# Attention with filler matmuls: when the fillers' inputs are loaded and split, where the softmax sums are gathered and exchanged, and when sums are evicted

## The chip, the cores and the metric

The kernel runs on one core of a Trainium2 chip. The metric is device time in microseconds (us) of one execution; the time before is the median of three runs. Five engines work side by side, each through its own instructions in order: PE (TensorE, matmuls), DVE (VectorE), ACT (ScalarE), POOL (GpSimd) and SP, which here only issues DMAs. They wait for one another by semaphores.

## The reference

One decoder layer of width 1024 over 2048 tokens, in float32:

```python
h = rms_norm(x, g_norm) * (1 + scale) + shift
x_rnn, z_rnn, q, k, v, z_attn, g_r, g_a = split(h @ w_in)
hr = rg_lru(causal_depthwise_conv(x_rnn), ...)              # linear recurrence over tokens
y_rnn = (hr * silu(z_rnn)) @ w_out_rnn
o = dilated_attention_mixture(rope(q), rope(k), v)          # 8 heads of 128
y_attn = (o * silu(z_attn)) @ w_out_attn
merged = sigmoid(g_r + b_r) * y_rnn + sigmoid(g_a + b_a) * y_attn
out = rms_norm(x + gate * (merged @ w_o), g_final)
```

Three causal attentions with (window, dilation) of (128, 1), (512, 4) and (2048, 16) are evaluated per head and added with the weights of their softmax sums: the result is one softmax over the three key sets together.

## The kernel before, in words

Float32 products are made of fast matmuls on split numbers: an operand is split into a rounded high part and the low part that is left, and `mm3` (L151) issues three matmuls (high by high, high by low, low by high). The high part is made by ACT (`hi_act`, L157) or DVE (`hi_dve`, L160), the low part by POOL (`lo_pool`, L163) or DVE (`lo_dve`, L166). A split so costs one instruction on each of two engines.

The first 1400 us or so compute the projections, the recurrence and the queries, keys and values. Then comes the attention stage, the place of the change, whose instruction order is written by hand (`tc.manual_schedule()`); behind it the last products follow, in an order that a scheduler sets.

**Units and slots.** The sequence is taken in two halves, f = 0 and f = 1, with 8 heads each: 16 heads in all. A head has six units (`ORDER`, L1392): four `c` units for the two wide windows, two `w` units for the narrow one. The loop runs over slots; slot s computes on PE the scores of unit s (tile `sc`, PSUM, two buffers), the transposes of unit s - 7 (`pT`, PSUM, two buffers), and the sums over values of unit s - 8 (`o`). In between:

- DVE adds the mask and takes the row minimum of the negated scores (L1470), ACT takes exponentials and sums them (L1471); minima and sums go into the small tile `st`.
- When a head's six units are scored, the two layouts of rows (g = 0 for `c`, g = 1 for `w`) must see each other's sums. `gather` (L1619) spreads `st` into `sm` on DVE, `exchange` is one small matmul `sc<-sm,msk` on PE into an `sc` buffer, `maxima`, `exponentials` and `weights` make the weights `M` on DVE and ACT. `scale` (L1535) then multiplies a unit's probabilities by `M` on ACT, in the slot before its transposes.
- The transposed probabilities are split into `pth` and `ptl` (L157 or L160, and L166). The sums in `o` are multiplied by the gate `zt` on their way out of PSUM by DVE (`evict`, L1594 for `c`, L1614 for `w`).

Within a slot the pieces are issued in this order: HEAD, scores and softmax steps, SOFTMAX, fillers, EXCHANGE, fillers, WEIGHTS, transposes, fillers, sums, TAIL. `at(slot, place, fn)` puts a function into one of the named places.

**Fillers.** Two output projections are cut into jobs of 64 steps (`steps`, L1707): jobs 0 to 3 are the recurrence's four column blocks, 4 to 7 the attention's. A step is one `mm3` with 512 columns into `pj`; eight steps (k = 0 to 7) make one tile, eight tiles (m = 0 to 7) a job. Each slot is owed 3.6 steps in the first half and 3.1 in the second, and `spend` issues whole steps until less than the allowance `left` + 1 is owed. A job needs eight inputs `y` of 128x512. `load_y` brings one from DRAM into a ring of four raw buffers (`R0` to `R3`), `split_y` makes `yh` and `yl` (nine buffers each). Loads of inputs 0 to 3 of the next job are issued at steps 44 to 50 of a job, those of 4 to 7 at steps 56 to 59, each for a buffer that the split of the input four before it frees; all eight splits are issued at steps 55 to 62. Weights come in halves of 512 KB (`S<-wD`).

Of the kernel before, what the change touches and what calls it, by code (L numbers as in the profile page):

```python
# [10 lines left out]
F32 = mybir.dt.float32  # L11
F32R = mybir.dt.float32r
# [77 lines left out]
def decoder_block(ctx, tc, x, c, positions, g_norm, w_mod, b_mod, w_in, b_gate, conv_w, conv_b,  # L90
# [4 lines left out]
    def T(pool, shape, dt, tag, **kw):  # L95
        cnt[0] += 1
        return pool.tile(shape, dt, tag=tag, name=f"{tag}_{cnt[0]}", **kw)
# [58 lines left out]
    def hi_act(o, i):  # L156
        nc.scalar.activation(o, i, AF.Copy)  # L157
# [182 lines left out]
    def load_yd(ys, n, k):  # L340
        x = n_y[0]
        n_y[0] += 1
        t = T(pR, [P, CH], F32, f"R{x % 4}")
        nc.sync.dma_start(t[:], ys[k * P : (k + 1) * P, n * CH : (n + 1) * CH])
        Y0[ys is yaT, n, k] = t
# [1054 lines left out]
    def at(slot, place, fn, *args):  # L1400
        plan.setdefault((slot, place), []).append((fn, args))
# [5 lines left out]
    class Head:  # L1407
# [208 lines left out]
            return evict  # L1616


        def gather(self):  # L1619

            self.sm = T(ap_, [P, 2, 4, 2, 8], F32, "sm")
            for g in range(2):
                nc.vector.tensor_tensor(
                    self.sm[:, g], self.st[:, :, g].rearrange("p t b n -> p t (b n)").unsqueeze(1).broadcast_to([P, 4, 2, 8]),
                    qm.unsqueeze(2).unsqueeze(3).broadcast_to([P, 4, 2, 8]), ALU.mult)

        def exchange(self):
            self.px = T(sc, [P, 2, 4, 2, 4, 2], F32, "sc")
# [52 lines left out]
        def enlist(self, B):  # L1681
            for c, (ld, s, place) in enumerate(((5, 2, HEAD), (5, 2, SOFTMAX), (4, 1, HEAD), (3, 0, HEAD))):
                at(B - ld, TAIL, self.load_kq, c)
                at(B - s, place, self.split_kq, c)
            for i, s in enumerate((B, B + 2)):
                at(s, HEAD, self.window_queries, i)
            e = B + NU
            at(e, HEAD, self.gather)
            at(e, EXCHANGE, self.exchange)
            at(e, EXCHANGE, self.maxima)  # L1690
            at(e, EXCHANGE, self.exponentials)
            at(e, WEIGHTS, self.weights)
            for u, (kind, x) in enumerate(ORDER):
                s = B + u + LAG
                at(s - 1, TAIL, self.scale, kind, x)
                at(s - 1, TAIL, self.split_v if kind == "c" else self.split_v1, x)
                at(s - 3, TAIL, self.load_v if kind == "c" else self.load_v1, x)
            e = B + NU + LAG
            at(B + LAG - 1, TAIL, self.load_gate)
            at(e, TAIL, self.merge, 1)  # L1700
            at(e + 1, TAIL, self.merge, 3)
            at(e + 2, TAIL, self.store)
# [4 lines left out]
    def steps(jobs):  # L1707

        tiles = [(j, m) for j in range(len(jobs)) for m in range(KT)]
        Y, G = {}, {}  # L1710

        def load_w(x):

            if x < 2 * len(tiles):
                assert x == n_w[0]
                j, m = tiles[x // 2]
                if not whole:
                    load_wd(jobs[j][0], m, x % 2)
                    return

                n_w[0] += 1
                W[x] = T(pS, [P, 2, KH, P], F32R, f"S{x % 4}")
                t = T(whole[0], [P, KH, P], F32, "wr", bufs=3)
                rows = slice(x % 2 * KH * P, (x % 2 + 1) * KH * P)
                nc.sync.dma_start(t[:], (w_out_rnn, w_out_attn)[jobs[j][0]][0, rows, m * P : (m + 1) * P]
                                  .rearrange("(k p) m -> p k m", p=P))
                hi_act(W[x][:, 0], t[:])
                (lo_dve if x % 2 else lo_pool)(W[x][:, 1], t[:], W[x][:, 0])

        def load_y(j, k):  # L1730
            if j < len(jobs):
                w, ys, n = jobs[j]
                if ys is oT and (n, k) == (2, KT - 1):

                    Y0[False, n, k] = last_head[0].zt[:, 0].rearrange("p r j -> p (r j)")
                    return
                assert ys is yaT or (n // 2, k, n % 2) in stored
                load_yd(ys, n, k)

        def split_y(j, k):  # L1740
            if j < len(jobs):
                Y[j, k] = yh, yl = [T(fl, [P, CH], F32R, tag, bufs=NY) for tag in ("yh", "yl")]
                w, ys, n = jobs[j]
                t = Y0.pop((ys is yaT, n, k))
                hi_act(yh[:], t[:])
                (lo_dve if k % 2 else lo_pool)(yl[:], t[:], yh[:])

        def load_g(t):
            j, m = tiles[t]
            w, ys, n = jobs[j]  # L1750
            at_ = slice(m * P, (m + 1) * P), slice(n * CH, (n + 1) * CH)
            G[t] = []
            for src in (grT,) if ys is yaT else (gaT, mrT):
                g = T(fl, [P, CH], F32, "fg", bufs=4)
                nc.sync.dma_start(g[:], src[at_])
                G[t].append(g)

        def evict(t, ps):
            g = G[t]
            nc.vector.tensor_tensor(g[0][:], ps[:], g[0][:], ALU.mult)  # L1760
            if len(g) > 1:
                nc.vector.tensor_tensor(g[0][:], g[0][:], g[1][:], ALU.add)  # L1762

        def store(t):
            j, m = tiles[t]
            w, ys, n = jobs[j]
            nc.sync.dma_start((mrT if ys is yaT else meT)[m * P : (m + 1) * P, n * CH : (n + 1) * CH], G.pop(t)[0][:])

        for k in range(KT):
            split_y(0, k)  # L1770
        yield
        last = None
        for t, (j, m) in enumerate(tiles):
            ps = T(pj, [P, CH], F32, "pj")
            for k in range(KT):
                if k % KH == 1:

                    load_w(2 * t + k // KH + 3)
                if k == 1 and t:
                    evict(t - 1, last)  # L1780
                if k == 3:
                    load_g(t)
                if k == 7 and t:
                    store(t - 1)
                wt = W[2 * t + k // KH]
                yh, yl = Y[j, k]
                mm3(ps[:], wt[:, 0, k % KH, :], wt[:, 1, k % KH, :], yh[:], yl[:], first=k == 0, last=k == KT - 1)
                if k % KH == KH - 1:
                    W.pop(2 * t + k // KH)

                step = m * KT + k
                if step in range(KT * KT - 20, KT * KT - 12, 2):
                    load_y(j + 1, (step - KT * KT + 20) // 2)
                if step == KT * KT - KT - 1:
                    split_y(j + 1, 0)
                if step >= KT * KT - KT and k + 1 < KT:
                    if k + 4 < KT:
                        load_y(j + 1, k + 4)
                    split_y(j + 1, k + 1)
                yield  # L1800
            last = ps
        evict(len(tiles) - 1, last)
        store(len(tiles) - 1)
# [13 lines left out]
    with tc.manual_schedule():  # L1817
        units = []
        for g in range(2 * H):
            hd = Head(g // H, g % H)  # L1820
            hd.enlist(NU * g)
            units += [(hd, u) for u in ORDER]
        last_head = [hd]
        owed = 0.0
        first = min(s for s, _ in plan)
        end = max(s for s, _ in plan) + 1
        for s in range(first, max(end, len(units) + LAG + 1)):
            rate = FILL[0] if s < NU * H + LAG else FILL[1]
            owed += rate + (MORE if 0 <= s <= NU else 0.0)

            run(s, HEAD)
            softmax = None
            if 0 <= s < len(units):
                hd, u = units[s]
                softmax = hd.scores(*u)
            if softmax:
                softmax()
            run(s, SOFTMAX)
            owed = spend(fill, owed, rate * 2 / 3)
            run(s, EXCHANGE)  # L1840
            owed = spend(fill, owed, rate / 3)
            run(s, WEIGHTS)
            if 0 <= s - LAG < len(units):
                hd, u = units[s - LAG]
                hd.transposes(*u)
            owed = spend(fill, owed, 0.0)
            if 0 <= s - LAG - 1 < len(units):
                hd, u = units[s - LAG - 1]
                evict = hd.sums(*u)
                if evict:  # L1850
                    at(s + 1, HEAD, evict)
            run(s, TAIL)
        owed = spend(fill, (NB + 2) * KT * KT - n_steps[0], 0)
    pools.close("ap", "sc", "pT", "po")
# [84 lines left out]
```

## Time and profile before

| | before |
|---|---|
| median of three runs (range) | 2293.89 us (2292.89 to 2299.7) |
| profiled execution, its own time | 2291.72 us |
| its span, first to last instruction | 2289.9 us |
| PE busy, share of the span | 2223.0 us, 97% |
| DVE | 1388.3 us, 61% |
| ACT | 1232.7 us, 54% |
| POOL | 993.6 us, 43% |
| granted PE clock, mean | 0.991 |

The profile is of one execution. A row of the timeline reads: start, duration, engine, line, operation, out<-in tiles, shapes, number of instructions merged; in brackets the engine's idle time before it and what ended it. PE overlaps matmuls, so the distance between two starts says what a matmul costs, not its duration. An engine that waits inside a merged row, or that is held up in the middle of an instruction, counts as busy.

### The profile page before, as it was taken

What the parts mean: (1) busy time and instruction counts of PE and PEld (TensorE: products, weight loads), DVE (VectorE), ACT (ScalarE), POOL (GpSimd) and SP (SyncE); (2) the same over time, 40 slices, a digit from 0 to 9 for tenths busy, and PEclk for the clock granted to TensorE, in tenths of its full rate; (3) what the DMA queues carried; (4) which work ended last, traced back from release to release, by engine and by line L of the source; (5) the groups of instructions that cost most, each with busy time, mean ns of one, the idle gap of its engine ahead of it and who ended that gap; (6) DMA issues with size and microseconds to landing.
All of it is one profiled execution on the core that took longest, in us unless ns stands there. A gap on an engine that the chain in (4) does not pass through costs nothing.

```text
span 2289.9 us, 34038 instructions
## 1 busy us (share of the span) xinstructions
PE 2223.0 (97%) x11455; PEld 1863.0 (81%) x11455; DVE 1388.3 (61%) x2380; ACT 1232.7 (54%) x2397; POOL 993.6 (43%) x742
## 2 busy tenths in 40 slices
PE   9999999999999999999999999999999998989998
PEld 5997788888777988888888877788888897868887
DVE  5668888768457555545445253567667777667443
ACT  3647768668433436557546312567677777533211
POOL 2367676767556432222222022446556556332100
PEclk9999999999999999999999999999999999999999
DMA  8367887887998458887888999889888888898542
GB/s 279 92 201 254 273 295 265 288 282 257 309 274 265 141 188 270 269 283 252 276 271 265 319 330 316 263 263 273 266 247 251 241 255 233 241 308 278 165 129 92
DMA packets 429011, 573.40 MB, mean 250 GB/s; under 512 B 72134, under 2 KB 293026, under 8 KB 427812
## 3 DMA queue, kind: packets, MB, share of 16 engines
q1 hardware_dynamic: 390996, 451.47, 64.4%
q10 hardware_dynamic: 37648, 119.70, 13.5%
q8 instruction: 91, 1.49, 0.3%
q14 instruction: 84, 0.69, 0.1%
q0 software_dynamic: 192, 0.05, 0.0%
HBM read 357.18 MB, written 213.91 MB: 249 GB/s over the span
## 4 chain that ended last, share of the span: by engine, by line
PE 56%; DMA 8%; DVE 3%; SPq 2%; ACT 2%; issue 1%; POOL 1%; ACTq 0%; POOLq 0%; DVEq 0%
PE pj L149 12%; PE X L149 8%; PE pq L149 8%; PE V L149 7%; PE o L149 4%; PE Z L149 4%; PE sc L149 4%; PE W L149 4%; PE Y L149 3%; DMA R<-in_w_in_dram 2%; DMA S<-sD 1%; PE pT L1555 1%; PE pg L149 1%; PE pT L1568 1%; DMA meT<-fg 1%
## 5 line engine op out<-in xcount | busy, mean ns | idle before, releaser
L149 PE MATMUL pj<-yh,S 128*128 128x512 f32 x1024 | 369.6, 405 | 6.6 <-DMA S<-wD 4.6
L149 PE MATMUL V<-T,S 128*128 128x512 f32 x1344 | 332.3, 396 | 6.4 <-DVE t L449 3.8
L149 PE MATMUL X<-T,S 128*128 128x512 f32 x1344 | 332.0, 396 | 3.8 <-ACT u L382 2.1
L163 POOL TENSOR_TENSOR S<-R,S 128x512 fp32r<-128x512 f32 x168 | 253.3, 1515 | 164.5 <-ACT S L157 145.2
L149 PEld LDWEIGHTS V<-T,S 128*128 128x128 f32 x1344 | 253.7, 189 | 67.1 <-issue 3.7
L149 PEld LDWEIGHTS X<-T,S 128*128 128x128 f32 x1344 | 253.4, 189 | 64.7 <-ACT u L382 2.8
L149 PEld LDWEIGHTS pj<-yh,S 128*128 128x128 f32 x1024 | 194.2, 190 | 44.3 <-DVE fg L1762 4.3
L149 PE MATMUL pj<-yl,S 128*128 128x512 f32 x512 | 202.5, 395 | 1.4 <-POOL yl L163 0.9
L1471 ACT ACTIVATE pp<-pp,st 128x256 f32<-128x256 f32 (+3 forms) x256 | 133.9, 524 | 107.4 <-DVE st L1470 106.7
L163 POOL TENSOR_TENSOR S<-s,S 128x512 fp32r<-128x512 f32 x84 | 131.9, 1571 | 127.4 <-ACT S L157 89.6
L149 PE MATMUL W<-T,S 128*128 128x512 f32 x672 | 165.8, 395 | 0.0
L149 PE MATMUL Z<-T,S 128*128 128x512 f32 x672 | 165.7, 395 | 0.0
L149 PE MATMUL Y<-T,S 128*128 128x512 f32 x672 | 165.5, 395 | 0.0
L163 POOL TENSOR_TENSOR s<-R,s 128x512 fp32r<-128x512 f32 x32 | 44.0, 1377 | 252.2 <-ACT s L157 193.9
L149 PEld LDWEIGHTS Y<-T,S 128*128 128x128 f32 x672 | 126.5, 188 | 29.4
L149 PEld LDWEIGHTS W<-T,S 128*128 128x128 f32 x672 | 126.1, 188 | 29.8 <-issue 0.9
L149 PEld LDWEIGHTS Z<-T,S 128*128 128x128 f32 x672 | 126.3, 188 | 29.3
L166 DVE TENSOR_TENSOR ptl<-pT,pth 128x384 fp32r<-128x384 f32 (+1 forms) x160 | 97.8, 628 | 65.7 <-ACT pth L157 63.5
L944 DVE SCALAR_TENSOR_TENSOR xc<-xr,par,xc 128x512 f32<-128x512 f32 x96 | 97.7, 1018 | 50.8 <-ACT xc L938 48.5
L1535 ACT ACTIVATE pp<-pp,M 128x256 f32<-128x256 f32 (+3 forms) x256 | 118.0, 523 | 9.0 <-DVE M L1659 9.0
L1470 DVE CUSTOM_DVE_ANT_0 pp<-sc,msk 128x256 f32<-128x256 f32 (+3 forms) x256 | 104.9, 449 | 25.6 <-PE sc L149 23.1
L157 ACT ACTIVATE S<-R 128x512 fp32r<-128x512 f32 x168 | 102.2, 621 | 21.8 <-DMA R<-in_w_in_dram 13.7
(331 smaller groups left out, 4763.4 us busy)
## 6 DMA issues: line engine op xcount, KB each, us to landing
sD<-S ACTq DMA_DIRECT2D x196, 512.0 KB, 4.0
S<-sD SPq DMA_DIRECT2D x196, 512.0 KB, 5.2
S<-wD SPq DMA_DIRECT2D x99, 512.0 KB, 5.7
R<-in_w_in_dram SPq DMA_DIRECT2D x136, 256.0 KB, 4.1
wD<-s ACTq DMA_DIRECT2D x64, 256.0 KB, 5.1
T<-in_w_mod_dram SPq DMA_DIRECT2D x8, 1024.0 KB, 11.4
vN<-ev SPq DMA_DIRECT2D x64, 128.0 KB, 1.9
zaT<-ev SPq DMA_DIRECT2D x32, 256.0 KB, 4.9
```

The costliest lines, as they stand in the source:

```text
L149: nc.tensor.matmul(o, lhsT=l, rhs=r, start=st, stop=sp, **kw)
L157: nc.scalar.activation(o, i, AF.Copy)
L163: nc.gpsimd.tensor_tensor(o, i, h.bitcast(F32), ALU.subtract)
L166: nc.vector.tensor_tensor(o, i, h.bitcast(F32), ALU.subtract)
L944: nc.vector.scalar_tensor_tensor(xc, xr[:, i : i + CH], cw(i), xc, ALU.mult, ALU.add)
L1470: nc.vector.tensor_tensor_reduce(pdst, s_ps, mask, 1.0, 3e38, ALU.add, ALU.min, m_)
L1471: nc.scalar.activation(pdst, pdst, AF.Exp, bias=m_, scale=-1.0, accum_out=l_)
L1535: nc.scalar.activation(pp, pp, AF.Copy, scale=w)
L1555: nc.tensor.transpose(pt[:, c0 + j * P : c0 + (j + 1) * P], pp[i][:, k * P : (k + 1) * P], ident)
L1568: nc.tensor.transpose(pt[:, c * P : (c + 1) * P], pp[:, half * P : (half + 1) * P], ident)
```

## The change

1. Inputs 0, 5, 6 and 7 of each job but the first are loaded straight into the buffer of their low part (`yl`); ACT reads it and writes `yh`, and the low part is made in place. Inputs 1 to 4 still go through `R`, so each raw buffer is used once in a job.
2. Loads of inputs 0 to 4 are issued at steps 40 to 48 of the job before, those of 5, 6, 7 in its last tile, behind k = 4, 5, 6. Splits 0 to 4 stay where they were; splits 5, 6, 7 move into the first tile of their own job, behind k = 0, 2, 3.
3. The eight low parts of job 0 are all made by DVE (four were POOL's).
4. `gather` takes one layout at a time: `w` behind the softmax steps of the head's last slot, `c` at the start of the next slot, where both were.
5. The evictions of `o` move from HEAD of the next slot to behind its softmax steps.
6. Three quarters of a slot's fillers come ahead of the exchange and the rest behind it; none are left between transposes and sums. Before, it was a third at each of the three places.

```diff
-            at(e, HEAD, self.gather)
+            at(e - 1, SOFTMAX, self.gather, 1)
+            at(e, HEAD, self.gather, 0)
...
+        def new_y(j, k):
+            Y[j, k] = [T(fl, [P, CH], F32R, tag, bufs=NY) for tag in ("yh", "yl")]
+            return Y[j, k]
...
-                load_yd(ys, n, k)
+                if k in (1, 2, 3, 4):
+                    load_yd(ys, n, k)
+                else:
+                    yh, yl = new_y(j, k)
+                    nc.sync.dma_start(yl[:].bitcast(F32), ys[k * P : (k + 1) * P, n * CH : (n + 1) * CH])
...
-                t = Y0.pop((ys is yaT, n, k))
-                hi_act(yh[:], t[:])
-                (lo_dve if k % 2 else lo_pool)(yl[:], t[:], yh[:])
+                t = Y0.pop((ys is yaT, n, k), None)
+                yh, yl = Y.get((j, k)) or new_y(j, k)
+                t = yl[:].bitcast(F32) if t is None else t[:]
+                hi_act(yh[:], t)
+                (lo_dve if k % 2 or not j else lo_pool)(yl[:], t, yh[:])
...
-                if step in range(KT * KT - 20, KT * KT - 12, 2):
-                    load_y(j + 1, (step - KT * KT + 20) // 2)
+                if step in range(KT * KT - 24, KT * KT - 14, 2):
+                    load_y(j + 1, (step - KT * KT + 24) // 2)
                 if step == KT * KT - KT - 1:
                     split_y(j + 1, 0)
-                if step >= KT * KT - KT and k + 1 < KT:
-                    if k + 4 < KT:
-                        load_y(j + 1, k + 4)
-                    split_y(j + 1, k + 1)
+                if m == KT - 1:
+                    if k < 4:
+                        split_y(j + 1, k + 1)
+                    elif k < KT - 1:
+                        load_y(j + 1, k + 1)
+                if j and m == 0 and k in (0, 2, 3):
+                    split_y(j, 5 + (k + 1) // 2)
...
             run(s, SOFTMAX)
-            owed = spend(fill, owed, rate * 2 / 3)
+            owed = spend(fill, owed, rate / 4)
             run(s, EXCHANGE)
-            owed = spend(fill, owed, rate / 3)
+            owed = spend(fill, owed, 0.0)
...
-                    at(s + 1, HEAD, evict)
+                    at(s + 1, SOFTMAX, evict)
```

How the instructions move is shown at three places, as the two kernels issue them.

ACT at the change from job 0 to job 1 (`yh` are the splits, `pp<-pp,M` the scaling that the next transposes wait for, `pp,st` the exponentials, `vh` and `kq` splits of values and keys). Before:

```order
L157 ACTIVATE yh_13356<-R_2301_13271 128x512
L157 ACTIVATE yh_13363<-R_2305_13283 128x512
L157 ACTIVATE yh_13372<-R_2311_13300 128x512
L157 ACTIVATE yh_13397<-R_2322_13354 128x512
L1535 ACTIVATE pp_12971<-pp_12971,M_13075 128x128
L1535 ACTIVATE pp_12971<-pp_12971,M_13075 128x256
L157 ACTIVATE vh_13409<-vraw_13239 128x256
```

And in the changed kernel:

```order
L157 ACTIVATE yh_13349<-R_2273_13137 128x512
L1535 ACTIVATE pp_12971<-pp_12971,M_13085 128x128
L1535 ACTIVATE pp_12971<-pp_12971,M_13085 128x256
L157 ACTIVATE vh_13399<-vraw_13240 128x256
L157 ACTIVATE kq_12675<-kraw_13242 128x512
L1471 ACTIVATE pp_13413,st_13050<-pp_13413,st_13050 128x128
L1471 ACTIVATE pp_13413,st_13050<-pp_13413,st_13050 128x256
L157 ACTIVATE yh_13356<-yl_13357 128x512
L157 ACTIVATE pth_13442<-pT_13438 128x384
```

Ahead of the same scaling stand the splits of inputs 4 to 7 before, and only that of input 4 now; input 5 follows one slot later, and 6 and 7 in the slot behind that.

DVE around a head's exchange in the second half (`sm` is the gather, `yw` and `y` the evictions of `o`, `pp,st<-sc` the softmax steps, `xq` the first step of the maxima). Before:

```order
L1760 TENSOR_TENSOR fg_17784<-pj_17706,fg_17784 128x512
L1762 TENSOR_TENSOR fg_17784<-fg_17784,fg_17786 128x512
L1623 TENSOR_TENSOR sm_17963<-st_17489,cs_60 128x64 x2
L1614 TENSOR_TENSOR yw_17823<-o_3285_17937,zt_17573 128x4x4x32
L1470 ISA pp_17981,st_17972<-sc_17973,msk_12673 128x384
L1470 ISA st_17972 128x1
L1470 ISA pp_17981,st_17972<-sc_17977,msk_12673 128x512
L1470 ISA st_17972 128x1
L1636 TENSOR_TENSOR xq_17991<-sc_17989,cs_60 128x64 x2
```

And in the changed kernel:

```order
L1772 TENSOR_TENSOR fg_17751<-fg_17751,fg_17753 128x512
L166 TENSOR_TENSOR ptl_17912<-pT_17906,pth_17911 128x512
L166 TENSOR_TENSOR ptl_17920<-pT_17915,pth_17919 128x384
L1623 TENSOR_TENSOR sm_17887<-st_17466,cs_60 128x64
L1470 ISA pp_17964,st_17955<-sc_17956,msk_12673 128x384
L1470 ISA st_17955 128x1
L1470 ISA pp_17964,st_17955<-sc_17960,msk_12673 128x512
L1470 ISA st_17955 128x1
L1614 TENSOR_TENSOR yw_17822<-o_3270_17923,zt_17553 128x4x4x32
L1636 TENSOR_TENSOR xq_17982<-sc_17980,cs_60 128x64 x2
```

One gather of two is left ahead of the softmax steps, and the eviction has moved behind them; the other gather stands one slot earlier.

PE in the same slot (`sc<-kq` scores, `sc<-sm` the exchange, `pj` filler steps, `pT` transposes, `o` sums). Before:

```order
L149 MATMUL sc_17977<-kq_12675 128x512 x3
L149 MATMUL pj_17909<-yh_17336,S_3232_17676 128x512
L149 MATMUL pj_17909<-yl_17337,S_3232_17676 128x512
L149 MATMUL pj_17909<-yh_17336,S_3232_17676 128x512
L149 MATMUL sc_17989<-sm_17963,msk_12673 128x128
L149 MATMUL pj_17909<-yh_17345,S_3232_17676 128x512
L149 MATMUL pj_17909<-yl_17346,S_3232_17676 128x512
L149 MATMUL pj_17909<-yh_17345,S_3232_17676 128x512
L1555 MATMUL pT_18015<-cs_60,pp_17409 128x128 x4
L1555 MATMUL pT_18024<-cs_60,pp_17409 128x128 x3
L149 MATMUL pj_17909<-yh_17374,S_3247_17757 128x512
```

And in the changed kernel:

```order
L149 MATMUL pj_17895<-yh_17328,S_3216_17660 128x512
L149 MATMUL pj_17895<-yl_17329,S_3216_17660 128x512
L149 MATMUL pj_17895<-yh_17328,S_3216_17660 128x512
L149 MATMUL sc_17980<-sm_17887,msk_12673 128x128
L149 MATMUL pj_17895<-yh_17337,S_3231_17741 128x512
L149 MATMUL pj_17895<-yl_17338,S_3231_17741 128x512
L149 MATMUL pj_17895<-yh_17337,S_3231_17741 128x512
L1555 MATMUL pT_18002<-cs_60,pp_17388 128x128 x4
L1555 MATMUL pT_18011<-cs_60,pp_17388 128x128 x3
L149 MATMUL o_3292_18019<-pth_17911,vh_17867 128x256
```

The exchange has two filler steps behind the scores instead of one (in other slots three), and the sums follow the transposes at once.

More of the change, by code (lines that the diff above doesn't have):

```diff
@@ L1616, in sums_w, with gather @@
             return evict
[L1619 to L1625, printed above, removed]
+        def gather(self, g):
+            if g:
+                self.sm = T(ap_, [P, 2, 4, 2, 8], F32, "sm")
+            nc.vector.tensor_tensor(
+                self.sm[:, g], self.st[:, :, g].rearrange("p t b n -> p t (b n)").unsqueeze(1).broadcast_to([P, 4, 2, 8]),
+                qm.unsqueeze(2).unsqueeze(3).broadcast_to([P, 4, 2, 8]), ALU.mult)
         def exchange(self):
@@ L1737, in load_y @@
                 assert ys is yaT or (n // 2, k, n % 2) in stored
-                load_yd(ys, n, k)
+                if k in (1, 2, 3, 4):
[3 more added lines that the diff above has]
+                    nc.sync.dma_start(yl[:].bitcast(F32), ys[k * P : (k + 1) * P, n * CH : (n + 1) * CH])
         def split_y(j, k):
             if j < len(jobs):
-                Y[j, k] = yh, yl = [T(fl, [P, CH], F32R, tag, bufs=NY) for tag in ("yh", "yl")]
                 w, ys, n = jobs[j]
-                t = Y0.pop((ys is yaT, n, k))
-                hi_act(yh[:], t[:])
-                (lo_dve if k % 2 else lo_pool)(yl[:], t[:], yh[:])
+                t = Y0.pop((ys is yaT, n, k), None)
[3 more added lines that the diff above has]
+                (lo_dve if k % 2 or not j else lo_pool)(yl[:], t, yh[:])
         def load_g(t):
```

## The prediction

> **What bounds the kernel now.** The page's first part, then the stretches of the attention stage:
>
> ```profile
> PE 2223.0 (97%) x11455; PEld 1863.0 (81%) x11455; DVE 1388.3 (61%) x2380; ACT 1232.7 (54%) x2397; POOL 993.6 (43%) x742
> 1430.00:1800.00 370.00, 354.19 (x2216) 313.68 (x2215) 241.89 (x737) 260.12 (x742) 204.20 (x189) 0.99 0.87 260
> 1800.00:2030.00 230.00, 216.10 (x1328) 189.56 (x1327) 159.22 (x359) 148.68 (x344) 114.74 (x87) 0.99 0.84 248
> ```
>
> PE is the bound, and the change neither adds nor removes a matmul. So it can only touch PE's gaps: 15.8 us idle in the first stretch, 13.9 in the second. Whatever it does on other engines counts only where PE waits for it. The list of PE's waits from 1425 to 2035 us says for whom (engine line <- releaser: total, times, longest):
>
> ```profile
> PE sc L149 <- DVE st L1470: 7.8, 4, 2.6
> PE pT L1555 <- ACT pp L1535: 7.5, 4, 5.6
> PE pT L1568 <- ACT pp L1535: 4.0, 2, 3.1
> PE pT L1555 <- DVE ptl L166: 3.9, 5, 1.6
> PE pj L149 <- DMA S<-wD: 3.9, 1, 3.9
> ...
> PE sc L149 <- DVE sm L1623: 0.6, 1, 0.6
> PE sc L149 <- POOL q L1432: 0.6, 2, 0.3
> ```
>
> Three kinds belong to the attention loop: transposes that wait for scaled probabilities (7.5 + 4.0), transposes that wait for a PSUM buffer (3.9), and the exchange, which waits for a score buffer or the gather (7.8 + 0.6); with the 0.6 for `q` they make 24.4 us. The wait for `S<-wD` lies behind the loop. Next I followed the longest one back through the timelines of SP, ACT and PE:
>
> ```profile
> 1474.34 0.38 SPq L344 DMA_DIRECT2D R<-yaT  x1
> 1473.91 0.64 ACT L157 ACTIVATE yh<-R 128x512 fp32r<-128x512 f32 x1 [1.89 <-DMA R<-yaT]
> 1475.87 1.34 ACT L157 ACTIVATE yh<-R 128x512 fp32r<-128x512 f32 x2 [1.32 <-DMA R<-yaT]
> 1479.44 0.63 ACT L157 ACTIVATE yh<-R 128x512 fp32r<-128x512 f32 x1 [2.23 <-DMA R<-yaT]
> 1479.97 0.78 ACT L1535 ACTIVATE pp<-pp,M 128x128 f32<-128x128 f32 x2
> 1480.41 1.09 PE L1555 MATMUL pT<-cs,pp 128*128 128x128 f32 x3 [5.55 <-ACT pp L1535]
> 1481.72 0.63 PE L149 MATMUL pj<-yl,S 128*128 128x512 f32 x1
> 1482.15 0.63 PE L149 MATMUL pj<-yh,S 128*128 128x512 f32 x1
> 1485.60 0.91 PE L149 MATMUL sc<-kq 128*128 128x128 f32 x6
> ...
> 1488.19 0.39 PE L149 MATMUL pj<-yl,S 128*128 128x512 f32 x1
> 1488.42 0.39 PE L149 MATMUL pj<-yh,S 128*128 128x512 f32 x1
> ...
> 1661.54 1.90 PE L1568 MATMUL pT<-cs,pp 128*128 128x128 f32 x8 [3.13 <-ACT pp L1535]
> 1666.79 0.40 PE L149 MATMUL pj<-yh,S 128*128 128x512 f32 x1
> ```
>
> This is the change from one filler job to the next. ACT, in order, stands three times (1.89 + 1.32 + 2.23 = 5.44 us) before splits whose input has not landed: the last load was issued at 1474.34, and its split started 5.1 us later. The scaling that PE needs is queued behind these splits. So the fillers, meant to hide the attention's waits, cause one. And the stall has a tail: from 1481.72 to 1482.15 a 512-column matmul takes 0.43 us against 0.23 at 1488.19, so PE ran slow from 1480.41 to about 1485.60. At 0.23/0.43 of its pace it loses 47% of 5.19 us, 2.4; after the wait of 3.13 us the same over 5.25 us (1661.54 to 1666.79), 2.4 more.
>
> The Trainium skill (TensorE: Matmul & The Clock Gate, Part 1) says that the array's clock halves after an idle window of about 3.4 us and returns after as long a busy one. The trace agrees on the halving, and shows it after 3.13 us of idling as well; by the page's window a tail would cost an estimated 1.7 us instead of 2.4, and the sum below would be 1.4 us smaller.
>
> The exchange's waits come from another place. PE, DVE and POOL at one of the two longest, and a gather that met nothing:
>
> ```profile
> 1818.05 0.49 PE L149 MATMUL sc<-sm,msk 128*128 128x128 f32 x2 [2.58 <-DVE st L1470]
> 1813.83 3.09 DVE L1623 TENSOR_TENSOR sm<-st,cs 128x64 f32<-128x64 f32 x2
> 1817.45 0.54 DVE L1470 CUSTOM_DVE_ANT_0 pp<-sc,msk 128x384 f32<-128x384 f32 x1
> 1849.82 0.35 DVE L1623 TENSOR_TENSOR sm<-st,cs 128x64 f32<-128x64 f32 x2
> 1813.49 1.59 POOL L163 TENSOR_TENSOR vh<-vraw,vh 128x512 fp32r<-128x512 f32 x1 [2.55 <-ACT vh L157]
> 1815.04 1.81 POOL L163 TENSOR_TENSOR kq<-kraw,kq 128x768 fp32r<-128x768 f32 x1
> ```
>
> Two tiny gathers took 3.09 us instead of 0.35, and ended with POOL's two splits (1815.08 and 1816.85). Behind them stood an eviction and then the softmax step whose end at 1817.99 freed the score buffer for the exchange.
>
> **The change part by part.** *Job changes.* Inputs 0 to 4 are loaded at least eleven steps ahead of their split, each into a raw buffer long free; 5, 6 and 7 now have four to five steps between load and split, instead of three, and the load waits for PE's last use of the buffer instead of another split. Some 96 slots lie in the two stretches' 600 us, about 6 us each with 3.1 to 3.6 steps, so four steps, which always cross into another slot, are 5 to 6.5 us by estimate, against 5.1 us for a landing. Input 5 may make ACT wait up to 1 us; 6 and 7 should not. Only five splits, not eight, stand together. Of the 11.5 us of waits on scaling I take 10.5 as gone, and both slow tails, 4.8. The 3.9 us of waits for `ptl` sit at the same changes, where DVE is late with low parts: 3.0 gone. What is next late there is the scaling itself, hidden by the filler steps that now all stand ahead of the transposes, one step (0.70 us) more than before. On SP three loads hold the queue until PE has passed their steps; behind them stand weights, keys and values, which are issued two slots ahead, so a hold of up to three steps (2.1 us) costs nothing unless they land 8 us late. I add 1.0 for input 5's remnant.
>
> *Exchange.* One or two more steps ahead of it (0.7 to 1.4 us), one gather less and the 0.7 us eviction no longer ahead of the softmax steps: on the rows above the softmax step would start when the first gather ends, near 1815.4, and the exchange finds its buffer free. Of 8.4 us I take 7.0 as gone. The chain behind it (maxima, weights, scaling) has a fifth of a step less before its transposes; nothing.
>
> By the Trainium skill (SBUF — State Buffer, Who interferes with whom) a DVE instruction with two SBUF inputs and a GpSimd one exclude each other for a whole instruction. The rows of 1813 to 1817 agree, and the rule speaks against part of the change: each gather, now in two places, can meet a POOL split of its own, and job 0's low parts all go to DVE. If one gather met a 1.81 us split at each long exchange, the sum would be an estimated 2 us smaller.
>
> *Evictions and order behind the softmax.* The rows that bear on what the eviction's move costs, PE and DVE in the slot after an exchange, and the small maxima step with and without POOL in its way:
>
> ```profile
> 1823.39 0.39 PE L149 MATMUL pj<-yh,S 128*128 128x512 f32 x1
> 1824.78 0.93 PE L1555 MATMUL pT<-cs,pp 128*128 128x128 f32 x7
> 1825.46 0.48 PE L149 MATMUL pj<-yh,S 128*128 128x512 f32 x1
> 1825.78 0.40 PE L149 MATMUL pj<-yl,S 128*128 128x512 f32 x1
> 1823.94 0.42 DVE L1470 CUSTOM_DVE_ANT_0 pp<-sc,msk 128x256 f32<-128x256 f32 x1
> 1827.80 0.69 DVE L1594 TENSOR_TENSOR zt<-o,zt 128x512 f32<-128x512 f32 x1 [0.60 <-PE o L149]
> 1781.31 1.32 DVE L1645 TENSOR_TENSOR M<-st,xs 128x16 f32<-128x16 f32 x1
> 1819.29 0.18 DVE L1645 TENSOR_TENSOR M<-st,xs 128x16 f32<-128x16 f32 x1
> ```
>
> Tight is only the last `c` eviction of a head: the next head's first sums want its single PSUM buffer at the end of the same slot. Scores end at 1823.39; three steps (0.70 each, from 1823.39 to 1824.78) and the transposes (0.68) put the sums 2.77 us later. DVE's last softmax step ends 0.97 later, an eviction of 0.69 makes 1.66: 1.1 us to spare. Where POOL holds up the maxima, as at 1781.31 (1.14 us over 0.18), the room is gone. Bounds: nothing, or all four steps and the eviction (4 x 0.42 + 0.69 = 2.4) at each of 15 heads, 36 us. I take 2.0, near the lower end, since DVE was on time in that slot.
>
> Sums directly behind transposes stand nowhere in this trace. A filler behind them takes 0.32 to its next start (1825.46) instead of 0.23; whether the sums pay that too, or not at all, or double, is 0.09 x 96 = 8.6 us either way. I take nothing and keep both ends.
>
> *Both ends of the loop.* Job 0's low parts on DVE save a wait on POOL:
>
> ```profile
> 1412.55 0.50 PE L149 MATMUL pj<-yl,S 128*128 128x512 f32 x1 [0.85 <-POOL yl L163]
> ```
>
> I take 0.8. Behind the loop the steps stand close together, so job 6's input 5 has nine steps (6.3 us) from load to use against 5.1 + 0.63 + a low part: it may be 1 us late, but the 3.9 us wait for `S<-wD` stands right behind and absorbs that. Nothing.
>
> Sum: 10.5 + 4.8 + 3.0 + 7.0 + 0.8 = 26.1 gone, 1.0 + 2.0 new: 23.1 us less. The profiled execution took 2291.72 us (span 2289.9), so 2268.6; the median of the runs, 2293.89, is 2.2 above it: 2271.
>
> **The rivals.** *Half.* Loads at the job changes still land late, and half of the 18.3 us there (10.5 + 4.8 + 3.0) stays: 2280. For it: 5.1 us of landing against 5 to 6.5. Against: only one input in eight is that tight.
>
> *The stall comes back whole.* SP's hold on the queue makes keys, values or weights late instead, or ACT waits on input 5 as long as it did: 23.1 - 18.3 = 4.8 us less, 2289. Then the change does not do at the job changes what it says. Against: those loads have two slots.
>
> *Slower: the eviction.* At each head's end PE waits for the PSUM buffer. At its full price, 36 us instead of 2, 2293.9 + 11 = 2305. It outweighs the gain from (26.1 - 1.0) / 15 = 1.7 us a head, that is with DVE 2.8 us later than in the rows above. For it: maxima held up by POOL. Against: that happens in some heads, and the exchange now comes later, when POOL's splits at the slot's start are further along.
>
> **How the numbers follow.** Forecast 0.66, half 0.14, whole stall 0.10, eviction 0.10. Below, all waits gone (24.4 + 4.8 + 0.8 = 30.0) with the 8.6 us gives 2255; above, half with most of the 8.6 us gives 2288. The range 2256 to 2288 leaves out the last two cases. A measurement can tell 0.3%, 6.9 us: faster is below 2287, so 0.80; the whole stall falls within, 0.10; slower 0.10.
>
> **What would show it.** In the changed profile ACT should wait for no load of `yl` or `R` over 1 us in the loop, PE's waits on `pp` and `ptl` should be under 2 us in all and no filler at 0.43 us stand inside it; the exchange should wait under 2 us in all. A new row "PE o <- DVE" of 15 or more waits would be the third rival; `pT` still waiting for `pp` at five places the first two. The forecast is wrong if the loop's idle time stays over 15 us, or if PE's busy time per slot changes.

## The result, and the profile after

The changed kernel took 2275.97 us (median of four runs, 2274.52 to 2278.36), the kernel before in the same comparison 2295.11: the ratio is 0.992, 95% interval 0.9904 to 0.9937. That is 19.1 us less, clear of the interval. The forecast was 23.1 less, 2271 us. The profiled executions stand 17.2 us apart (2291.72 and 2274.52).

Where the 17.2 lie is read from the first and last start of four tiles. These are rows of the groups by tile, first of before, then of after (tile, count, shortest/mean/longest ns, first to last start):

```profile
L149 PE MATMUL pj<-yh,S x1024: 387/393/776, 1408.4 to 2194.1; 128*128 128x512 f32 x171
L149 PE MATMUL sc<-kq x384: 221/337/415, 1425.0 to 1958.9; 128*128 128x128 f32 x64, 128*128 128x384 f32 x64, 128*128 128x256 f32 x32, 128*128 128x512 f32 x32
L149 PE MATMUL o<-pth,vh x384: 220/281/415, 1461.7 to 1998.7; 128*128 128x256 f32 x128, 128*128 128x128 f32 x64
L149 PE MATMUL pq<-oh,mh x256: 389/389/792, 2034.1 to 2280.7; 128*128 128x512 f32 x128
```

```profile
L149 PE MATMUL pj<-yh,S x1024: 387/392/793, 1411.5 to 2177.0; 128*128 128x512 f32 x171
L149 PE MATMUL sc<-kq x384: 220/335/628, 1426.6 to 1942.3; 128*128 128x128 f32 x64, 128*128 128x384 f32 x64, 128*128 128x256 f32 x32, 128*128 128x512 f32 x32
L149 PE MATMUL o<-pth,vh x384: 220/282/419, 1463.2 to 1981.9; 128*128 128x256 f32 x128, 128*128 128x128 f32 x64
L149 PE MATMUL pq<-oh,mh x256: 389/389/398, 2019.0 to 2263.6; 128*128 128x512 f32 x128
```

From the first score (`sc`) to the last sum (`o`) the loop took 573.7 us and takes 555.3: 18.4 less. Around it little moved: the fillers start 3.1 later (a stage that the change does not touch), the stretch from there to the first score is 1.5 shorter, the one from the last sum to the first `pq` 1.7 longer, and the rest 2.1 shorter. Of the 3.1, more time at a lower granted clock accounts for 1.7: up to the first score this cost 8.5 us in before and 10.2 in after (sum over stretches of 5 us of 5 x (1 - granted clock)). The gain is the loop's.

The page's first row of after, which answers to the one of before:

```profile
PE 2220.0 (98%) x11454; PEld 1864.4 (82%) x11455; DVE 1382.2 (61%) x2384; ACT 1230.5 (54%) x2397; POOL 990.9 (44%) x738
```

And the list of PE's waits of after from 1420 to 2020 us (total, times, longest):

```profile
PE pj L149 <- ACT S L157: 5.3, 1, 5.3
PE sc L149 <- POOL q L1432: 2.7, 5, 0.9
PE pj L149 <- ACT yh L157: 2.6, 1, 2.6
PE pT L1555 <- ACT pp L1535: 2.3, 2, 2.0
PE sc L149 <- DVE sm L1623: 1.9, 2, 1.7
PE sc L149 <- DVE xq L1636: 1.4, 1, 1.4
PE pj L149 <- DMA S<-wD: 1.0, 1, 1.0
PE pj L149 <- POOL yl L163: 0.9, 1, 0.9
PE pT L1555 <- DVE ptl L166: 0.7, 1, 0.7
PE o L149 <- DVE zt L1594: 0.4, 1, 0.4
```

The waits on `S` and `yh` lie behind the loop, the one on `S<-wD` ahead of the first score. What is left, 10.3 us, is the loop's, against 24.4 before. By busy time the same: in the loop PE stood idle for 24.8 us and now does for 10.8; the other 4.4 of the 18.4 are busy time, 3.4 of them clock (below). At the first job change the chain starts as before, with ACT at a load that has not landed, and then goes another way (timelines of SP, ACT, DVE and PE):

```profile
1475.28 0.38 SPq L1747 DMA_DIRECT2D yl<-yaT  x1
1481.07 0.63 ACT L157 ACTIVATE yh<-yl 128x512 fp32r<-128x512 f32 x1 [3.40 <-DMA yl<-yaT]
1481.73 0.69 DVE L166 TENSOR_TENSOR yl<-yl,yh 128x512 fp32r<-128x512 f32 x1 [3.43 <-ACT yh L157]
1483.40 0.56 DVE L1623 TENSOR_TENSOR sm<-st,cs 128x64 f32<-128x64 f32 x1
1484.02 0.49 PE L149 MATMUL sc<-sm,msk 128*128 128x128 f32 x2 [1.67 <-DVE sm L1623]
1486.33 1.70 DVE L166 TENSOR_TENSOR yl<-yl,yh 128x512 fp32r<-128x512 f32 x1 [1.21 <-ACT yh L157]
1487.95 0.34 DVE L1636 TENSOR_TENSOR xq<-sc,cs 128x64 f32<-128x64 f32 x2
1488.44 0.96 PE L149 MATMUL sc<-kq,q 128*128 128x256 f32 x6 [1.40 <-DVE xq L1636]
```

ACT still stands 3.40 us before a load, but PE has its filler steps ahead of it and no longer waits for the scaling behind that split. It meets the delay later and smaller: the low part, and behind it on DVE the gather, come late, and the exchange waits 1.67. Then PE stops a second time, at a place where it did not before. A low part of one of the last inputs, moved into this tile, stands on DVE ahead of the first step of the maxima (`xq`). DVE waits 1.21 us for its high part and takes 1.70 for it, where the low part above took 0.69; a low part on POOL runs from 1486.20 to 1487.48 beside it. The next scores need the buffer that `xq` reads, and wait 1.40.

### The profile page after: what moved, and what is told of

It is laid out like the page before. It is cut to its first block, busy times and chain, and to the rows that moved or that the text cites. A ratio compares the mean times of both kernels' runs of the same rounds, so it can differ in the third digit from the quotient of the medians.

```text
span 2272.7 us, 34029 instructions
## 1 busy us (share of the span) xinstructions
PE 2220.0 (98%) x11454; PEld 1864.4 (82%) x11455; DVE 1382.2 (61%) x2384; ACT 1230.5 (54%) x2397; POOL 990.9 (44%) x738
## 3 DMA queue, kind: packets, MB, share of 16 engines
q10 hardware_dynamic: 37648, 119.70, 13.7%
## 4 chain that ended last, share of the span: by engine, by line
PE 59%; DMA 6%; DVE 3%; ACT 2%; SPq 2%; issue 1%; POOL 1%; ACTq 0%; POOLq 0%; DVEq 0%
PE pj L149 12%; PE X L149 8%; PE pq L149 8%; PE V L149 8%; PE W L149 4%; PE Z L149 4%; PE sc L149 4%; PE o L149 4%; PE Y L149 3%; DMA R<-in_w_in_dram 2%; PE pT L1555 1%; PE pg L149 1%; PE pT L1568 1%; DMA R<-yaT 1%; SPq L252 1%
## 5 line engine op out<-in xcount | busy, mean ns | idle before, releaser
L149 PE MATMUL pj<-yh,S 128*128 128x512 f32 x1024 | 344.7, 397 | 9.0 <-ACT S L157 5.3
L163 POOL TENSOR_TENSOR kq<-kraw,kq 128x512 fp32r<-128x512 f32 (+1 forms) x64 | 101.2, 1592 | 41.7 <-ACT kq L157 32.1
```

Source lines behind the costliest of these rows:

```text
L149: nc.tensor.matmul(o, lhsT=l, rhs=r, start=st, stop=sp, **kw)
L163: nc.gpsimd.tensor_tensor(o, i, h.bitcast(F32), ALU.subtract)
```

## The experiments

Four letters name the parts: **L** the loads and splits of the job changes (parts 1 and 2, with job 0's low parts), **G** the gather in two, **V** the evictions behind the softmax steps, **O** the order of the fillers. L + G + V + O is the changed kernel. All were timed in five rounds against the kernel before, on three occasions; each ratio is to the times of before from its own occasion.

**L alone.** The diff of the change without these lines:

```diff
-            at(e, HEAD, self.gather)
+            at(e - 1, SOFTMAX, self.gather, 1)
+            at(e, HEAD, self.gather, 0)
-            owed = spend(fill, owed, rate * 2 / 3)
+            owed = spend(fill, owed, rate / 4)
-            owed = spend(fill, owed, rate / 3)
+            owed = spend(fill, owed, 0.0)
-                    at(s + 1, HEAD, evict)
+                    at(s + 1, SOFTMAX, evict)
```

> The kernel before with parts 1 and 2 alone (direct loads, earlier loads, splits 5 to 7 in their own job, job 0's low parts on DVE); gather, evictions and filler order stay. Theory (ACT stood in order before late loads, and the scaling behind it): about 16 us of the 19 are here: waits on pp 9.2, slow-clock tails 4.8, waits on ptl 3.2, less 0.9 for a late low part; 2277 to 2283 us, and PE's waits on pp in the loop under 4 us. Rival (the filler steps that now stand ahead of the transposes hide the scaling): the waits on pp stay above 7 us and the time above 2288.

2291.6 us, ratio 0.999 (0.9978 to 1.0002). The theory is right on the waits on `pp` and wrong on the time; the rival the other way round. PE's waits in the loop:

```profile
PE sc L149 <- DVE st L1470: 9.8, 4, 3.9
PE sc L149 <- DVE sm L1623: 2.6, 1, 2.6
PE pT L1555 <- ACT pp L1535: 1.4, 3, 0.8
PE pT L1555 <- DVE ptl L166: 1.3, 2, 0.7
PE pT L1568 <- ACT pp L1535: 0.8, 2, 0.5
```

DVE and PE at the exchange of 1812, from the timeline:

```profile
1808.26 3.09 DVE L1623 TENSOR_TENSOR sm<-st,cs 128x64 f32<-128x64 f32 x2
1812.48 0.67 PE L149 MATMUL sc<-sm,msk 128*128 128x128 f32 x2 [2.58 <-DVE st L1470]
```

And the stretches behind the longest of these waits (busy time of PE, PEld, DVE, ACT and POOL, then PE's granted clock, 0.53 and 0.79):

```profile
1925.00:1930.00 5.00, 3.49 (x13) 3.09 (x14) 4.01 (x17) 2.16 (x6) 1.41 (x3) 0.53 0.58 164
1930.00:1935.00 5.00, 5.00 (x31) 4.62 (x31) 2.24 (x9) 2.76 (x8) 2.54 (x2) 0.79 0.50 159
```

The exchange now waits 12.4 us instead of 8.4, also at two job changes, where before it waited 0.4 at most, and each of its four longest waits is followed by a lower granted clock, which costs 1.7, 1.7, 1.8 and 3.4 us. So of the 11.9 us that the job changes' waits lost, 4.0 came back at the exchange and 3.5 as slow clock. The loop of this execution is still 5.0 us shorter than before's; the whole is only 1.2 shorter, as its first score comes 3.0 later. By the medians L alone gains 2.0 us, and the interval reaches to 5.0: that most of the gain is handed back is shown, that all of it is, is not.

**G, V and O without L**, the same lines without parts 1 and 2, and **O alone**:

> The kernel before with everything but parts 1 and 2: gather in two, evictions behind the softmax steps, three quarters of the fillers ahead of the exchange, none behind the transposes. Theory: the exchange's 8.4 us of waits shrink by about 5, the long waits on pp by one filler step (0.7 us) each; 2288 to 2293 us, and ACT still waits 4 to 6 us for R at the job changes. Rival (filler order hides the scaling): under 2284, waits on pp under 4 us.

> The kernel before with the two spend lines alone: three quarters of a slot's steps ahead of the exchange, a quarter ahead of the transposes, none between transposes and sums. Theory: one more step ahead of four long exchange waits and six waits on pp, 0.7 us each at most, and nothing for sums directly behind transposes: 2289 to 2294. Rival (filler order is the gain): under 2284. If the sums directly behind transposes cost or save 0.09 us in each of 96 slots, the time lies 8.6 us higher or lower than that.

2292.62 us, ratio 0.9998 (0.9984 to 1.0012), and 2293.69 us, 1.0004 (0.9989 to 1.0018). The times lie at the upper ends of the theories' ranges, but the sizes behind them were not foreseen: the exchange's waits fall further, to 1.6 and 2.3, and the job changes' rise. PE's waits with O alone:

```profile
PE pT L1555 <- DVE ptl L166: 13.1, 5, 6.4
PE pT L1568 <- ACT pp L1535: 4.4, 2, 3.8
PE sc L149 <- DVE st L1470: 2.3, 1, 2.3
PE pT L1555 <- ACT pp L1535: 2.0, 2, 1.8
```

Its first job change on DVE and PE:

```profile
1480.79 0.69 DVE L166 TENSOR_TENSOR yl<-R,yh 128x512 fp32r<-128x512 f32 x1 [2.49 <-ACT yh L157]
1482.95 0.87 PE L1555 MATMUL pT<-cs,pp 128*128 128x128 f32 x3 [6.42 <-DVE ptl L166]
```

DVE stands before a low part whose high part ACT has not made, and behind it are the `ptl` that free the transposes' buffers. That these stalls grow because all of a slot's splits now come ahead of its transposes is argued from the order, not shown. Slow clock grew as well, from 5.1 to 13.7 us.

The second half of the expectation on O alone is answered by PE's starts: the first sum of a slot behind a filler in before, then behind the transposes in after.

```profile
1461.68 0.28 PE L149 MATMUL o<-pth,vh 128*128 128x256 f32 x1
1461.80 0.28 PE L149 MATMUL o<-ptl,vh 128*128 128x256 f32 x1
1485.28 0.36 PE L149 MATMUL o<-pth,vh 128*128 128x256 f32 x1
1485.49 0.28 PE L149 MATMUL o<-ptl,vh 128*128 128x256 f32 x1
```

A first sum takes 0.12 us to the next start behind a filler and 0.20 behind transposes (medians of some 60 places in the loop, both of 256 columns). A filler paid 0.09 at that place before (0.32 instead of 0.23) and no longer stands there. The sums took over the fillers' price, and the two together hardly moved.

**The changed kernel without O**, and then **without G**, and **without V**:

> The changed kernel with before's filler order alone. Theory: 1 to 4 us over the changed kernel (2277 to 2280), from the exchange and the scaling, which have a step less ahead of them. Rival (filler order is the gain): 10 us or more over it, 2286 or more, with waits on pp back above 7 us.

> The changed kernel with both gathers at HEAD of the exchange's slot, as before. Theory (loads alone gained only 2 us because DVE, late at the exchange, then stops PE there, and the gather that POOL holds up is what makes it late): the exchange's waits return to 8 to 12 us, 2282 to 2288. Rival (it is the eviction ahead of the softmax steps that makes DVE late): within 2 us of the changed kernel.

> The changed kernel with the evictions back at HEAD, ahead of the softmax steps. Theory (the gather is what makes DVE late): 0 to 3 us over the changed kernel. Rival (the eviction is): 2282 to 2288, with waits of the exchange on st of 6 us or more.

2277.52 us (0.9927, 0.9908 to 0.9946), 2274.38 us (0.9908, 0.989 to 0.9926) and 2276.78 us (0.9917, 0.9899 to 0.9935). The theory held for O and V, the rival for G: none of the three is needed by itself. With O in place, to undo the gather or the eviction leaves the exchange's waits at 2.0 and 4.4 us, against 3.3, so the question of who makes DVE late was put where O already covers it.

**The splits closer to their loads.** Inputs 5 to 7 of the changed kernel are split two steps behind their loads:

```diff
+                    if k >= KT - 2:
+                        split_y(j + 1, k - 1)
-                if j and m == 0 and k in (0, 2, 3):
-                    split_y(j, 5 + (k + 1) // 2)
+                if j and m == 0 and k == 0:
+                    split_y(j, 7)
```

> The changed kernel with the splits of inputs 5, 6 and 7 only two steps behind their loads (behind k = 6 and 7 of the last tile and k = 0 of the next) instead of four or five. Theory (ACT standing in order before a load that has not landed stops the scaling and the softmax steps behind it): each job change gives 2 to 3 us of waits back, on pp, st or ptl, 2283 to 2290, and ACT's waits for yl in the loop rise from 5.8 to 15 us or more. Rival (where DVE's work stands is all that counts, not ACT's waits): within 3 us of the changed kernel.

2288.06 us, ratio 0.9971 (0.9957 to 0.9985): 12 us over the changed kernel, as the theory expected. ACT's waits for these loads from 1420 to 1990 us, those of the second projection behind those of the first:

```profile
ACT yh L157 <- DMA yl<-yaT: 15.5, 4, 6.5
ACT yh L157 <- DMA yl<-oT: 5.6, 1, 5.6
```

The first job change on SP and ACT:

```profile
1479.20 0.38 SPq L1747 DMA_DIRECT2D yl<-yaT  x1
1484.63 0.63 ACT L157 ACTIVATE yh<-yl 128x512 fp32r<-128x512 f32 x1 [6.51 <-DMA yl<-yaT]
```

And PE's waits:

```profile
PE pT L1555 <- ACT pp L1535: 11.7, 7, 4.6
PE pT L1555 <- DVE ptl L166: 7.1, 2, 6.4
```

ACT stood ready at 1478.12, before the load was even issued. Two to three steps less between load and split bring back waits of 18.8 us on `pp` and `ptl`, against 15.4 before, and that costs most of what the change gains. (The profiled execution took 2294.41 us, 6.4 more than the median.)

**L with one helper each**: O, G or V.

> The changed kernel with both the gather and the evictions as before: parts 1 and 2 and the filler order alone. Theory (with the loads on time, what is left is the exchange, late by one to two steps, and either the filler order or gather and evictions cover it): 2274 to 2279, waits of the exchange on st and sm under 4 us in all. Rival (the filler order needs the lighter DVE at the slot's start as well): 2284 or more, with these waits over 8 us.

> Parts 1 and 2 and the gather in two; evictions and filler order as before. Theory (without the filler order it is the gather, held up by POOL, that makes DVE late at the exchange): near the kernel that has evictions and gather, 2277 to 2281, exchange waits about 7 us. Rival (it is the eviction): near the loads alone, 2287 to 2292, exchange waits 10 us or more.

> Parts 1 and 2 and the evictions behind the softmax steps; gather and filler order as before. Theory (the gather is what makes DVE late): near the loads alone, 2287 to 2292. Rival (it is the eviction): 2277 to 2281.

2279.09 us (0.9941, 0.9922 to 0.9959), 2281.85 us (0.9952, 0.9935 to 0.9969) and 2281.58 us (0.9953, 0.9936 to 0.997). The first theory held for the waits (3.4 us on `st` and `sm`) and for the time just not; on who makes DVE late neither theory nor rival held. G's time just misses the theory's range, and its exchange waits, 11.5 us, are the rival's; V's time just misses its rival's. O beside L gains by itself; G and V beside L each gain about 0.4% over L alone, and alike, so neither the gather nor the eviction alone makes DVE late. They stand in one row on DVE. To take one out took 0.9 (G) and 2.3 us (V) off the exchange's waits and 3.6 and 5.2 off the slow clock; that this is all of their gain is not shown.

**Two attempts at less.** Inputs 5 to 7 through raw buffers and the last key chunk split a slot earlier; then, besides, five weight halves ready-made:

```diff
-                if k in (1, 2, 3, 4):
+                if k:
-                    elif k < KT - 1:
-                        load_y(j + 1, k + 1)
+                    if 2 <= k < 5:
+                        load_y(j + 1, k + 3)
-  ... (4, 1, HEAD), (3, 0, HEAD)
+  ... (4, 1, HEAD), (4, 1, SOFTMAX)
-                if not whole:                    # the second kernel only
+                if not whole or x < 104:
```

> The changed kernel with inputs 5 to 7 loaded through the raw buffers that splits 1 to 3 free, behind k = 2 to 4 of the last tile (two steps earlier, and three ahead of where the yl buffers come free), and with the last key chunk split one slot earlier, so that the query casts on POOL start sooner. Theory: ACT's waits for yl in the loop (5.8 us) and PE's on q (2.7) mostly go; 2 to 6 us less than the changed kernel, 2270 to 2274. Rival (the loads now wait on SP for the split's low part and hold up keys and weights): 2276 or more, with ACT's waits on kraw over 12 us.

> The changed kernel with inputs 5 to 7 through the raw buffers, the last key chunk split a slot earlier, and the first five weight halves behind the attention loop loaded ready-made (S<-wD) instead of raw and split on the chip. Theory: PE's wait of 5 us on a weight split behind the loop goes, and with it a stretch at half clock (1.7 us); 3 to 7 us under the same kernel without it (2274): 2267 to 2271. Rival (512 KB halves land as late as 256 KB ones and their split together): 2273 or more, with a wait on S<-wD of 4 us or more in its place.

2273.97 us (2272.82 to 2274.49; ratio 0.9905, 0.9884 to 0.9926) and 2274.3 us (0.9919, 0.99 to 0.9939). The first, at the upper end of its theory's range, did to ACT and POOL what it should (ACT's waits on loads of inputs in the loop 1.2 instead of 5.8 us, PE's on `q` 0.7 instead of 2.7), but one late low part took 2.4 us back, in PE's waits of the first:

```profile
PE pj L149 <- POOL yl L163: 2.4, 1, 2.4
```

In the second the wait on a weight split became one on the weight itself, as its rival said:

```profile
PE pj L149 <- DMA S<-wD: 5.3, 3, 4.7
```

The intervals of these ratios overlap that of the changed kernel: no version here is shown to beat it.

**The account of all runs.** Loop: first score to last sum. Job changes: PE's waits on `pp` and `ptl`. Exchange: on `st`, `sm` and `xq`. Half clock: sum over the loop's stretches of 5 us of 5 x (1 - granted clock), part of which falls into the waits. Above, this is the slow clock.

| parts | ratio to before | loop, us | job changes | exchange | half clock |
|---|---|---|---|---|---|
| none (before) | 1 | 573.7 | 15.4 | 8.4 | 5.1 |
| O | 1.0004 | 577.8 | 19.5 | 2.3 | 13.7 |
| G V O | 0.9998 | 575.0 | 18.0 | 1.6 | 11.8 |
| L | 0.999 | 568.7 | 3.5 | 12.4 | 8.6 |
| L G | 0.9952 | 565.6 | 3.5 | 11.5 | 5.0 |
| L V | 0.9953 | 560.9 | 3.1 | 10.1 | 3.4 |
| L G V | 0.9927 | 561.3 | 2.9 | 7.2 | 5.1 |
| L O | 0.9941 | 557.8 | 3.0 | 5.3 | 1.8 |
| L G O | 0.9917 | 557.1 | 3.2 | 4.4 | 0.0 |
| L V O | 0.9908 | 552.7 | 3.0 | 2.0 | 0.0 |
| L G V O (after) | 0.992 | 555.3 | 3.0 | 3.3 | 1.7 |
| after, splits closer to loads | 0.9971 | 571.9 | 18.8 | 1.5 | 10.2 |
| after, raw buffers | 0.9905 | 554.4 | 2.7 | 2.6 | 1.7 |
| the same, ready-made weights | 0.9919 | 554.0 | 2.7 | 3.7 | 1.7 |

The job changes' waits go with L, the exchange's with O and less with G and V, and each alone raises the other column or the half clock. Taking all of the loop's waits and its half clock from its length leaves 540 to 545 us in every row, with either filler order: no other cost above some 5 us is left. One profile stands for each row, and the loop of a single execution can lie some us from the typical one: those of L G V, L G and the splits closer to loads stand for executions that took 5.7, 3.0 and 6.4 us more than the median of their kernel, that of L V for one of 4.0 less.

## Why the prediction came out as it did

**The bound and the place** were right: PE's matmuls are unchanged, and the loop is 18.4 us shorter, 14.0 of it in PE's idle time and 3.4 in the clock. The time came out within the range, 5 us above the forecast.

**The sizes, term by term.** Waits on scaling: 11.5 to 2.3, so 9.2 gone (taken 10.5). Waits on `ptl`: 3.9 to 0.7, 3.2 gone (3.0). Slow clock: 5.1 to 1.7 by the granted clock, 3.4 gone (4.8); this one is in part luck, since whether a wait is followed by slow clock differs from one execution to the next (last section). Exchange: 8.4 to 3.3, 5.1 gone (7.0). Job 0: 1.5 up to the first score (0.8). New: 2.1 more on `q`, 0.9 for a low part on POOL, 0.4 for the gate, 3.4 in all (3.0, but for other things, so that this term is right by luck). That makes 19.0 less, where the start of the fillers and the loop together shrank by 19.9. The forecast's 23.1 was too large by the terms for exchange, scaling and clock, which assumed that nearly everything would go; the stage ahead, 3.1 longer, accounts for the rest of the distance in the profiled executions.

**What failed is the assignment of the gain to the edits.** The working put the job changes' 18.3 us down to the loads and splits and 7.0 to the exchange's own edits, as if each brought its own. For the whole change that sum held within 4 us; for its parts it does not. The runs show 2 us for L alone and nothing for the rest alone, within their intervals, and 19 together. At a job change both kinds of wait are the end of one late chain (a split on ACT, a low part on DVE, and behind these `ptl`, gather and softmax steps). PE, released from one, meets the other: two of L's four longest waits at the exchange stand at job changes, where before it waited 0.4 at most. Waits of either kind can also bring slow clock. The question "what is late next there" was answered with the scaling, and the answer was the exchange.

**Input 5's remnant** was taken as up to 1 us of ACT's time. ACT stood 3.40 us, and what it cost PE was the 1.67 at the exchange. For inputs 6 and 7 nothing was taken; a low part of theirs ahead of `xq` cost 1.40 more. The load issued at 1475.28 landed by 1481.07, 5.8 us where 5.1 was taken. The larger error is the distance: four steps were turned into 5 to 6.5 us by PE's pace, but steps order only PE. ACT ends its work ahead of that split 3.40 us before 1481.07, at 1477.67, and so stood there 2.4 us after the issue.

**The exchange's mechanism** was half right. A gather of one piece can still be held up by POOL:

```profile
1765.46 1.88 DVE L1623 TENSOR_TENSOR sm<-st,cs 128x64 f32<-128x64 f32 x1
1765.41 1.84 POOL L163 TENSOR_TENSOR kq<-kraw,kq 128x768 fp32r<-128x768 f32 x1
```

A gather further on, at 1768.92, took 0.21. The held-up one stands behind the softmax steps, and no wait of PE follows from it. So a gather that stands alone does meet a POOL split, as the forecast weighed, but the 2 us set against it (the working does not say how 1.81 us at each long exchange make 2) did not show: without the split of the gather the kernel is no slower. What did show is the low part of 1.70 us ahead of `xq`. Given L, the filler order alone takes the exchange's waits from 12.4 to 5.3 us, gather and evictions without it to 7.2.

**Evictions and adjacency.** For the evictions 2.0 was taken, with 36 as the upper bound: PE waited 0.4 us once for the gate, and undoing the move changes nothing that can be told. For sums directly behind transposes nothing was taken, and nothing came: they pay 0.08 us each, and the fillers' 0.09 at that place is gone.

**Behind the loop** nothing was taken, and the two stretches there make -0.4; but not by the reason given. Before, 3.9 + 1.5 + 2.6 us of waits on weights and on `mh` stood there. In their place stand 2.6 on a late input (`yh`, where 1 was put as possible) and 5.3 on `S`, nearly the same in all; why the second has this length was not tested.

**The rivals.** None of the three came in the changed kernel. L alone takes about the time of the whole stall coming back (2291.6 against 2289), but through the exchange and not through SP's queue. The half-rival's mechanism, loads that still land late, is there in small (ACT's 3.40 us), and in full in the kernel with the early splits (2288, where 2280 was put). Of the signs named, waits of ACT over 1 us, 3.0 us on `pp` and `ptl`, 3.3 at the exchange and one stretch at half clock inside the loop missed their bounds; the loop's idle time, 10.8 us, stayed under 15, PE's busy time there went from 548.9 to 544.5 us, of which 3.4 is clock, and no row "PE o <- DVE" with many waits came.

## What to carry to other kernels

When several waits hang on one late chain of in-order engines, do not add the gains of the edits that remove them: ask for each edit alone which wait PE meets next, and expect little while that one is uncovered. A load that an in-order engine splits needs its full landing time in steps between issue and split; the cost of two to three steps less was 12 us here. When an edit gains nothing, look whether its own wait is gone and another has grown before you drop it.

## What the runs showed of the hardware

Half-clock stretches follow waits of one length in one run and not in another. In before the wait of 2.58 us that ended at 1818.05 had none; its stretch:

```profile
1815.00:1820.00 5.00, 2.42 (x16) 1.80 (x15) 4.66 (x13) 1.62 (x6) 2.95 (x4) 1.00 0.72 219
```

In the kernel with L alone the wait of 2.58 that ended at 1812.48 had one (granted clock 0.76 and 0.89 in the two stretches of 5 us from 1810). In after, one followed a wait of only 2.05, on PE's timeline:

```profile
1884.53 0.30 PE L1555 MATMUL pT<-cs,pp 128*128 128x128 f32 x1 [2.05 <-ACT pp L1535]
```

and the stretch behind it:

```profile
1885.00:1890.00 5.00, 4.90 (x25) 4.77 (x26) 2.83 (x11) 5.00 (x16) 2.65 (x3) 0.66 0.23 70
```

A granted clock of 0.66 over 5 us is 1.7 us lost. The four events of L alone lost 1.7, 1.7, 1.8 and 3.4 us, the two of before 3.4 and 1.7: about that or twice it. The Trainium skill (TensorE: Matmul & The Clock Gate, Part 1) describes a free-running window of 3.4 us, which agrees with this chance and with the 1.7 us (half of it); its threshold, a whole idle window, does not agree with a wait of 2.05.

Such events go with the spread of a kernel's times: in 29 runs of the kernel before, the fastest (2287.12 us) had a mean granted clock of 0.992, the slowest (2302.03) of 0.987, and 0.005 of 2290 us is 11 us of the 15 between them. The clock is not all of it: a run of 2288.74 us had 0.989.
